# A seven-product feed-forward on one Trainium2 core: PSUM banks, weight sums and modulation steps in another order

## The chip, the core and the metric

The kernel runs on one core of a Trainium2 chip. Its engines are TensorE (PE), VectorE (DVE), ScalarE (ACT), GpSimd (POOL) and SyncE (SP), each with an instruction stream of its own; semaphores order them. The metric is the device time of one execution in microseconds. The kernel before took 2130.96 us, the median of three runs from 2126.84 to 2132.02.

## The reference

Two layers, each a half feed-forward, a token mixer, and a second half feed-forward, over 256 latent and 256 context tokens with a model width of 1024 (the last two blocks on the latent tokens alone):

```
swiglu(h, w1, w3, w2) = (silu(h @ w1) * (h @ w3)) @ w2          # 1024 -> 2816 -> 1024
m = (silu(c) @ w_ada[l] + b_ada[l]) in 9 vectors of 1024         # mc likewise, from c_ctx
x = x + 0.5 * m[2] * swiglu(modulate(rms_norm(x), m[0], m[1]), ...)      # feed-forward 0
x = x + m[5] * token_mixer(modulate(rms_norm(x), m[3], m[4]), ...)
x = x + 0.5 * m[8] * swiglu(modulate(rms_norm(x), m[6], m[7]), ...)      # feed-forward 1
```

Everything is float32. The kernel computes a product from a rounded part (hi) and a rest (lo) of either factor: hi x hi, hi x lo and lo x hi.

## The kernel before, in words

**Products.** Activations lie transposed, channels on partitions and tokens along the free axis. A weight block of 512 rows by 256 columns is loaded (512 KB, L297) by SP into one of a few raw buffers, cast to `whi` by ACT (L324), and `wlo` = raw - `whi` is formed by DVE (L325). Three matmuls of 128x256 follow per 128x128 piece.

**Feed-forward over 512 tokens.** `ffn_both` runs three times: layer 0 first, layer 0 second, layer 1 first. Its 11 column blocks of w1 and w3 are done as follows: block 0 in the entry before it, blocks 1 and 2 by `ordinary`, blocks 3 to 10 by `seven`, in groups of one, four and three, each group followed by `down` blocks (products with w2). The `seven` function computes a w1 block and a w3 block together, with seven half-size products instead of eight in the manner of Strassen. Such a pair is seven units, 0 to 6, of 24 matmuls each (L753), 24 pairs in all. The weights of the units are a11, s1, s2, a12, s3, s4, a22: three raw blocks, two sums which the DMA forms (s1 and s3, loaded by SP at L725 and accumulated by POOL's queue at L726), and two sums which DVE forms (s2 = s1 + a11 and s4 = s2 + a12, L739).

**Banks of a pair.** The units write the PSUM banks b, c, b, a, b, c, b. Between them a bank is read: ACT keeps b after unit 0 (q1), c after unit 1 (p5) and b after unit 2 (w1), all at L758; DVE adds a to q1 after unit 3, b to p5 after unit 4 and c to w1 after unit 5 (L761); after unit 6 DVE gates (L776). Banks b and c are two halves of one tile `p1`; a is half of a tile `p3`. Dependencies are tracked per tile.

**Order.** The function `pipeline` writes the order of PE, DVE and ACT out by hand. Per unit it emits: evacuations of the unit before (`now`); loads, and casts and subtractions of units up to four ahead (`prep`, where also the two sums stand); pieces of finished modulation vectors (`finish`); modulation steps; ACT's silu or the cast of a finished pair (`end`); then the unit's matmuls. There are five raw buffers, of which units hold at most three at a time.

**Modulation steps.** A vector of `m` and `mc` is computed beside the products by the generator `ada`: eight steps, each a 512 KB load (L224) and two DVE operations that accumulate weights times the two conditioning vectors (L240; the first step L238). Then `ada_end` sums over partitions with four ones-matmuls (L253), copies the row (L257), transposes it (L260) and adds the bias (L262). Steps are spread by each unit's `cost`: 0.14 for a pair's unit, 0.6 for a unit of the second ordinary block, 0.3 per 128 rows in `down`. `ffn_both` does 32, 40 and 40 steps in its three runs. The first `down` block of the first two runs has a `need`: the eight steps of the first vector must be done before its residual add.

**The last feed-forward** (`ffn`, 256 tokens) takes its products one after the other, in an order which the scheduler makes.

Of the kernel before, what the change touches and what calls it, by code (L numbers as in the profile page):

```python
# [79 lines left out]
def dit_kernel(ctx: ExitStack, tc: tile.TileContext, I: dict, out: bass.AP):  # L80
# [44 lines left out]
    xr = [z0[:, t * D:(t + 1) * D] for t in range(3)] + [z1[:, 0:D]]  # L125
    junk, dg = z1[:, D:2 * D], z1[:, 2 * D:2 * D + 512].rearrange("p (t c) -> p t c", t=4)
    c32 = z1[:, 2 * D + 512:2 * D + 768].rearrange("p (k c) -> p k c", k=KD)
    qrow, ms4 = z1[:, 2 * D + 768:2 * D + 896], z1[:, 2 * D + 896:2 * D + 908].rearrange("p (a t) -> p a t", a=3)
    last_wada = half_zone(0)[:, 0:D].rearrange("p (k m c) -> p k m c", k=2, m=2)
# [119 lines left out]

    def ada_end(l, m, acc, pool):  # L250
        pa = psum_bg(f"pa{l}_{m}")
        for q in range(4):
            te.matmul(pa[32 * q:32 * q + 32, 0, :], ones32, acc[:, q % 2, (q // 2) * 512:(q // 2 + 1) * 512],  # L253
                      start=True, stop=True, tile_position=(0, 32 * q))
        yield
        mrow = pool.tile([P, 512], F32, tag="mrow", name="mrow")
        v.tensor_copy(mrow, pa[:, 0, :])  # L257
        yield
        for b in range(4):
            te.transpose(pa[:, 1, b * P:(b + 1) * P], mrow[:, b * P:(b + 1) * P], ident)  # L260
        yield
        v.tensor_tensor(modT[l][:, m].rearrange("p (h b) t -> p h b t", h=2),  # L262
                        pa[:, 1, :].rearrange("p (b h t r) -> p h b t r", b=4, h=2, t=2)[:, :, :, :, 0],
                        biasT[l][:, 8 * m:8 * m + 8].rearrange("p (h b) -> p h b", h=2).unsqueeze(3)
                        .to_broadcast([P, 2, 4, 2]), ALU.add)
        modulated(l, m)

# [345 lines left out]
    class Unit:  # L613


        def __init__(self, mm, prep, load=None, takes=0, gives=0, now=(), end=(), cost=1.0, need=None):
            self.mm, self.prep, self.load, self.takes, self.gives = mm, prep, load, takes, gives
            self.now, self.end, self.cost, self.need = now, end, cost, need

    def pipeline(units, fills, steps, total, made):  # L620

# [16 lines left out]
        with tc.manual_schedule(engines={eng.PE, eng.DVE, eng.Activation}):  # L638
            for i in range(len(units) + 1):
# [8 lines left out]
                while pi < min(len(units), i + 4):  # L648
                    while li < len(units) and (li <= pi or out + units[li].takes <= 3):
                        if units[li].load:  # L650
                            units[li].load()
                        out += units[li].takes
                        li += 1
                    units[pi].w = units[pi].prep()
                    out -= units[pi].gives
                    pi += 1
                for f in fills.get(i, ()):
                    f()
                finish()
                if i < len(units):  # L660
                    want += units[i].cost * scale
                    while did < min(total, int(want + 1e-6)) and step():
                        did += 1
                if prev:
                    for f in prev.end:
                        f()
                if i < len(units):
                    units[i].mm(units[i].w)
# [44 lines left out]
    def seven(fm, wa, wb, c0, fp, done):  # L713
# [22 lines left out]
        def summed(name, a, b):  # L736
            def prep():
                x[name] = fm.sum_place()
                v.tensor_tensor(x[name], x[a], x[b], ALU.add)  # L739
                return split(x[name], 4, 2 * P)  # L740
            return prep

        def part(bank, form, first=False):
            def mm(wt):
                if bank == "b" and first:
                    x["q1"], x["p5"], x["w1"] = fm.places()
                    pab, pc = psum("p1"), psum_bg("p3")
                    x["b"], x["c"], x["a"] = pab[:, 0], pab[:, 1], pc[:, 0]
                for k in range(4):
# [23 lines left out]
        def gate(h, by):  # L773
# [4 lines left out]

        cost = 0.14
        return [  # L780
            Unit(part("b", fm.b11, True), whole("a11"), first_loads, 1, 0, [keep("q1", "b")], cost=cost),
            Unit(part("c", fm.t1, True), whole("s1"), None, 0, 0, [keep("p5", "c")], cost=cost),
            Unit(part("b", fm.t2), summed("s2", "s1", "a11"), None, 0, 1, [keep("w1", "b")], cost=cost),
            Unit(part("a", fm.b21, True), whole("a12"), raw("a12", wa, 1), 1, 0, [add("q1", "a")], [silu(0, "q1")], cost=cost),
            Unit(part("b", fm.t3), whole("s3"), None, 0, 0, [add("p5", "b")], cost=cost),
            Unit(part("c", fm.b22), summed("s4", "s2", "a12"), None, 0, 1, [add("w1", "c")], [silu(1, "w1")], cost=cost),
            Unit(part("b", fm.t4), whole("a22"), raw("a22", wb, 1), 1, 1, [gate(0, "b"), gate(1, "p5")],
                 [lambda: done(x["gt"])], cost=cost)]

    def ffn_both(l, f, norm, mods, then, first):  # L790

# [4 lines left out]
        with tc.tile_pool(name=f"ffn{l}{f}", bufs=1) as fp:  # L796
# [27 lines left out]
            def ordinary(c):  # L824
# [17 lines left out]
                for n, (w, name) in enumerate(((w1, "p1"), (w3, "p3"))):  # L842
                    for i in range(2):
                        more = {"cost": 0.6 if c > 1 else 0}
# [6 lines left out]
                return us  # L851

            def down(cg, r0, kt, last, need):
# [18 lines left out]
                for k in range(0, kt, 4):  # L872
                    n = min(4, kt - k)
                    more = {"cost": 0.3 * n}
                    if k + n == kt:
                        more.update(now=[added], end=[stats] if last else [], need=need)
                    us.append(chunk(w2, r0 + k, n, cg * 2 * P, acc, k == 0, k + n == kt,
                                    lambda k=k: (g["hi"], g["lo"], k), **more))
                return us

# [15 lines left out]
            with norm.done():  # L896
                pipeline(units, fm.fills, ada(mods, fp, made), KD * len(mods), made)
# [4 lines left out]
    def ffn(l, f, norm, then):  # L902

# [3 lines left out]
        with tc.tile_pool(name=f"ffn{l}{f}", bufs=1) as fp:  # L907
            def weights(n):
                return [tuple(fp.tile([P, 4, 2 * P], F32R, name=f"e{i}{x}") for x in ("hi", "lo")) for i in range(n)]

            for g0, g1 in ((0, 6), (6, 11)):
                ghi, glo = (zone(i, F32R).rearrange("p (k n) -> p k n", k=12) for i in range(2))
                for g in range(g0, g1):
# [613 lines left out]
```

## Time and profile before

| | |
|---|---|
| median of three runs | 2130.96 us |
| profiled execution, its own time | 2139.14 us |
| its span, first to last instruction | 2137.4 us |
| PE busy | 1978.2 us (93%) |
| DVE busy | 1580.8 us (74%) |
| ACT busy | 962.6 us (45%) |
| mean granted TensorE clock | 0.979 |
| moved by DMA | 326.49 MB, mean 153 GB/s |

The profile is of one execution, and its times are relative to the span's start. Busy time counts an engine with any instruction under way. A granted clock of 1 is 2.4 GHz and of 0.5 is 1.2 GHz. In the timelines a matmul's length overlaps the next one's, so the time per matmul is read from the distance of their starts. The idle time in square brackets is what an engine waited before an instruction, with the instruction that released it.

### The profile page before, as it was taken

The page shows a single profiled execution, that of the slowest core. Times are in us where ns is not written, and L with a number is a line of the kernel's source. Part 1 is how long each engine was busy: PE and PEld are TensorE (multiplying, and loading weights), DVE is VectorE, ACT ScalarE, POOL GpSimd, SP SyncE. Part 2 cuts the span into 40 slices and gives each one's busy share as a digit, 9 for nine tenths or more (in the row PEclk, how much of TensorE's full clock was granted, in tenths as well). Part 3 has the DMA queues.
Part 4 walks back from the last instruction along what each step waited for, and adds up shares of the span by engine and source line. Part 5 has one row for each costly group of instructions (what it writes and reads, how often), then busy time and mean ns, then how long its engine had stood idle before and what let it go on. Part 6 is the DMA issues. An engine that isn't in the chain of part 4 may idle for free. (4 is left out here: it accounts for less than half of the span.)

```text
span 2137.4 us, 32048 instructions
## 1 busy us (share of the span) xinstructions
PE 1978.2 (93%) x12743; PEld 1733.8 (81%) x12743; DVE 1580.8 (74%) x2338; ACT 962.6 (45%) x1466; POOL 116.4 (5%) x80
## 2 busy tenths in 40 slices
PE   8979898899999999998889899988988999999998
PEld 6768887788777778876887778777878798899998
DVE  6776776767678877787678777776877769967555
ACT  3423423356466533531432444324334567766443
POOL 1100100000001110000000000000000000110000
PEclk8989999999999999999999999999999999999999
DMA  8765765432212545665677365766763333455663
GB/s 296 209 165 156 171 198 137 121 120 83 79 57 88 164 149 162 159 177 165 164 194 197 94 183 118 213 163 164 210 160 116 89 98 114 142 172 180 186 188 108
DMA packets 278542, 326.49 MB, mean 153 GB/s; under 512 B 15520, under 2 KB 260344, under 8 KB 278136
## 3 DMA queue, kind: packets, MB, share of 16 engines
q1 hardware_dynamic: 253048, 299.27, 45.3%
q0 software_dynamic: 25344, 25.17, 8.1%
q8 instruction: 100, 1.64, 0.3%
q14 instruction: 50, 0.41, 0.1%
HBM read 321.25 MB, written 3.15 MB: 152 GB/s over the span
## 5 line engine op out<-in xcount | busy, mean ns | idle before, releaser
L324 ACT CAST whi<-wraw 128x1024 fp32r<-128x1024 f32 (+2 forms) x371 | 369.8, 1000 | 569.9 <-PE py L320 220.2
L325 DVE TENSOR_TENSOR wlo<-wraw,whi 128x1024 fp32r<-128x1024 f32 (+2 forms) x343 | 403.2, 1178 | 193.6 <-ACT whi L324 188.7
L240 DVE SCALAR_TENSOR_TENSOR aacc<-wada,cs,aacc 128x1024 f32<-128x1024 f32 x224 | 280.4, 1298 | 4.6 <-DMA wada<-w_ada 4.5
L753 PE MATMUL p<-hhi_f,whi 128*128 128x256 f32 x768 | 222.3, 289 | 47.4 <-DVE half L761 26.4
L753 PE MATMUL p<-zone,whi 128*128 128x256 f32 x1152 | 212.8, 287 | 43.1 <-ACT half L758 43.1
L753 PEld LDWEIGHTS p<-zone,whi 128*128 128x128 f32 x1152 | 179.7, 194 | 52.7 <-ACT half L758 52.7
L319 PE MATMUL p<-hhi_f,whi 128*128 128x256 f32 (+1 forms) x672 | 216.2, 322 | 2.3 <-DVE hhi_f L392 2.3
L753 PE MATMUL p<-hlo_f,whi 128*128 128x256 f32 x768 | 217.3, 283 | 0.0
L753 PE MATMUL p<-hhi_f,wlo 128*128 128x256 f32 x768 | 217.0, 283 | 0.0
L321 PE MATMUL p<-hhi_f,wlo 128*128 128x256 f32 (+1 forms) x672 | 215.0, 320 | 1.1 <-DVE wlo L325 0.6
L320 PE MATMUL p<-hlo_f,whi 128*128 128x256 f32 (+1 forms) x672 | 215.5, 321 | 0.5 <-DVE hlo_f L397 0.2
L753 PEld LDWEIGHTS p<-hhi_f,whi 128*128 128x128 f32 x768 | 148.4, 193 | 62.4 <-DVE half L761 31.1
L319 PE MATMUL py<-ghi,whi 128*128 128x512 f32 x492 | 194.4, 395 | 0.0
L320 PE MATMUL py<-glo,whi 128*128 128x512 f32 x492 | 192.8, 392 | 0.6 <-DVE glo L325 0.5
L321 PE MATMUL py<-ghi,wlo 128*128 128x512 f32 x492 | 192.1, 391 | 0.0
L753 PE MATMUL p<-zone,wlo 128*128 128x256 f32 x576 | 162.7, 282 | 0.0
L753 PEld LDWEIGHTS p<-hlo_f,whi 128*128 128x128 f32 x768 | 148.6, 194 | 0.2
L753 PEld LDWEIGHTS p<-hhi_f,wlo 128*128 128x128 f32 x768 | 148.6, 193 | 0.0
L319 PEld LDWEIGHTS p<-hhi_f,whi 128*128 128x128 f32 x672 | 128.5, 191 | 14.0 <-issue 3.5
L321 PEld LDWEIGHTS p<-hhi_f,wlo 128*128 128x128 f32 x672 | 127.0, 189 | 12.1 <-POOL wlo L325 1.2
L320 PEld LDWEIGHTS p<-hlo_f,whi 128*128 128x128 f32 x672 | 127.2, 189 | 11.6 <-DVE hlo_f L397 1.6
L319 PE MATMUL pg<-hhi_m,whi 128*128 128x512 f32 (+1 forms) x384 | 132.2, 344 | 0.0
(363 smaller groups left out, 4381.3 us busy)
## 6 DMA issues: line engine op xcount, KB each, us to landing
wraw<-ffn_w SPq DMA_DIRECT2D x232, 512.0 KB, 4.2
wada<-w_ada SPq DMA_DIRECT2D x128, 512.0 KB, 3.6
wraw<-w_in SPq DMA_DIRECT2D x64, 512.0 KB, 3.5
s<-ffn_w SPq DMA_DIRECT2D x48, 512.0 KB, 5.2
s<-ffn_w POOLq DMA_DIRECT2D x48, 512.0 KB, 6.8
wraw<-w_out SPq DMA_DIRECT2D x16, 512.0 KB, 3.5
wada<-w_ada SPq DMA_DIRECT2D x30, 256.0 KB, 5.7
wraw<-w_in SPq DMA_DIRECT2D x16, 384.0 KB, 3.3
```

The costliest lines, as they stand in the source:

```text
L240: v.scalar_tensor_tensor(acc[:, t], w, cs[:, k, t:t + 1], acc[:, t], op0=ALU.mult, op1=ALU.add)
L319: te.matmul(o, a, xh, start=start, stop=False)
L320: te.matmul(o, a, xl, start=False, stop=False)
L321: te.matmul(o, b, xh, start=False, stop=stop)
L324: s.copy(hi, src)
L325: eng.tensor_tensor(lo, src, hi.bitcast(F32), ALU.subtract)
L753: te.matmul(om, wt[w][:, k, cm], form[f][:, k], start=(first and k == m == n == 0), stop=(k == 3 and m == 1 and n == 2), skip_group_check= ...
```

## The change

The following is done at once.

- In a pair bank b has a tile `p1` of its own, and c and a are the halves of tile `p3`.
- The two sums of a pair are no longer part of `prep`: they are emitted as `first` in the slot after the units of that slot were prepared, so one slot ahead of their cast.
- In a slot `end` of the unit before stands ahead of the steps. In a pair only unit 2 has a cost (1), the second ordinary block's units have 1, `down` 0.22 per 128 rows.
- `ada_end` yields twice before its ones-matmuls.
- A `down` block with `need` hands its residual add to the first unit of the next block.
- The runs of `ffn_both` do 32 steps each. Vector (1,7) is computed on PE in the third run by the new `ada_apart`, with two of its steps per slot: fp32 matmuls of the two conditioning columns with the weights, at four column positions. Vector (1,8) is done in the last feed-forward, one step after each product.

```diff
     def ada_end(l, m, acc, pool):
+        yield
+        yield
         pa = psum_bg(f"pa{l}_{m}")
...
+    def ada_apart(l, m, pool, made):
+        pa = psum_bg(f"pa{l}_{m}")
+        v.memset(pa[:, 0, 0:L], 0.0)
+        ahead = ada_load(l, m, 0)
+        yield
+        for k in range(KD):
+            w, ahead = ahead, ada_load(l, m, k + 1) if k + 1 < KD else None
+            for q in range(4):
+                te.matmul(pa[32 * q:32 * q + 2, 0, 0:L], cs[:, k], w[:, q * L:(q + 1) * L],
+                          start=(k == 0), stop=(k == KD - 1), tile_position=(0, 32 * q))
+            if k == KD - 1:
+                made.append(ada_apart_end(l, m, pa, pool))
+            yield
+
+    def ada_apart_end(l, m, pa, pool):
+        mrow = pool.tile([P, 512], F32, tag="mrow", name="mrow")[:, 0:L]
+        v.tensor_copy(mrow, pa[:, 0, 0:L])
+        yield
+        for b in range(2):
+            te.transpose(pa[:, 1, b * P:(b + 1) * P], mrow[:, b * P:(b + 1) * P], ident)
+        yield
...
@@ pipeline
+                if pi < len(units) and units[pi].first:
+                    units[pi].first()
                 for f in fills.get(i, ()):
                     f()
                 finish()
+                if prev:
+                    for f in prev.end:
+                        f()
                 if i < len(units):
                     want += units[i].cost * scale
                     while did < min(total, int(want + 1e-6)) and step():
                         did += 1
-                if prev:
-                    for f in prev.end:
-                        f()
-                if i < len(units):
+                    for _ in range(2):
+                        next(apart, None)
                     units[i].mm(units[i].w)
@@ seven
         def summed(name, a, b):
-            def prep():
+            def add():
                 x[name] = fm.sum_place()
                 v.tensor_tensor(x[name], x[a], x[b], ALU.add)
-                return split(x[name], 4, 2 * P)
-            return prep
+            return add
...
-                    pab, pc = psum("p1"), psum_bg("p3")
-                    x["b"], x["c"], x["a"] = pab[:, 0], pab[:, 1], pc[:, 0]
+                    pb, pac = psum("p1"), psum_bg("p3")
+                    x["b"], x["c"], x["a"] = pb[:, 0], pac[:, 0], pac[:, 1]
...
-        cost = 0.14
+        cost = 0
...
-            Unit(part("b", fm.t2), summed("s2", "s1", "a11"), None, 0, 1, [keep("w1", "b")], cost=cost),
+            Unit(part("b", fm.t2), whole("s2"), None, 0, 1, [keep("w1", "b")], cost=1, first=summed("s2", "s1", "a11")),
...
-            Unit(part("c", fm.b22), summed("s4", "s2", "a12"), None, 0, 1, [add("w1", "c")], [silu(1, "w1")], cost=cost),
+            Unit(part("c", fm.b22), whole("s4"), None, 0, 1, [add("w1", "c")], [silu(1, "w1")], cost=cost,
+                 first=summed("s4", "s2", "a12")),
@@ down, in ffn_both
-                    more = {"cost": 0.3 * n}
-                    if k + n == kt:
-                        more.update(now=[added], end=[stats] if last else [], need=need)
+                    more = {"cost": 0.22 * n}
+                    if k + n == kt and need is None:
+                        more.update(now=[added], end=[stats] if last else [])
...
+                if need is not None:
+                    late.append((added, need))
+                elif late:
+                    us[0].now, us[0].need = [late[0][0]], late.pop()[1]
@@ ffn
                             product(acc, load(w, KD, g * 2 * P), (hhi, hlo), L)
+                            with norm.done():
+                                background(1)
@@ the blocks
-    ffn_both(0, 1, after, [(0, 8)] + [(1, m) for m in range(4)], entry, True)
+    ffn_both(0, 1, after, [(0, 8)] + [(1, m) for m in range(3)], entry, True)
...
-    ffn_both(1, 0, entry, [(1, m) for m in range(4, 9)], after, False)
+    ffn_both(1, 0, entry, [(1, m) for m in range(3, 7)], after, False, (1, 7))
...
-    ffn(1, 1, entry, Output())
+    ffn(1, 1, entry, [(1, 8)], Output())
```

The first place where the order differs is PE's stream in a pair of the first feed-forward. The rows are the first matmuls of units 0 to 6, with what each writes (`p1` or `p3`) and reads; the rest of a unit is left out.

Before:

```order
L753 MATMUL p1_2955<-hhi_f00_129,whi_2843 128x256 [waits Activation_49]
...
L753 MATMUL p1_2955<-zone0_614,whi_2874 128x256 [waits Activation_49]
...
L753 MATMUL p1_2955<-zone0_614,whi_2904 128x256 [waits Activation_49]
...
L753 MATMUL p3_2956<-hhi_f00_129,whi_2947 128x256 [waits PE_49]
...
L753 MATMUL p1_2955<-zone0_614,whi_2982 128x256 [waits Activation_49]
...
L753 MATMUL p1_2955<-hhi_f00_129,whi_3012 128x256 [waits DVE_49]
...
L753 MATMUL p1_2955<-hhi_f00_129,whi_3043 128x256 [waits DVE_49,Activation_49]
```

After:

```order
L785 MATMUL p1_2955<-hhi_f00_129,whi_2847 128x256 [waits Activation_49]
...
L785 MATMUL p3_2956<-zone0_614,whi_2878 128x256 [waits Activation_49]
...
L785 MATMUL p1_2955<-zone0_614,whi_2908 128x256 [waits Activation_49]
...
L785 MATMUL p3_2956<-hhi_f00_129,whi_2947 128x256 [waits Activation_49]
...
L785 MATMUL p1_2955<-zone0_614,whi_2982 128x256 [waits Activation_49]
...
L785 MATMUL p3_2956<-hhi_f00_129,whi_3012 128x256 [waits DVE_49]
...
L785 MATMUL p1_2955<-hhi_f00_129,whi_3047 128x256 [waits DVE_49,Activation_49]
```

Six of the seven units wrote the tile `p1`; now the units write `p1` and `p3` in turn.

The second place is DVE's stream from the end of this pair into the next: `half` and `w1` are the places of the kept banks and of the sums, `aacc` the accumulator of a modulation vector.

Before:

```order
L761 TENSOR_TENSOR half1_617<-p1_2955,half1_617 128x512 [waits PE_49]
L325 TENSOR_TENSOR wlo_3106<-s1_2939,whi_3105 128x1024 [waits DMASW6_49,Activation_49]
L761 TENSOR_TENSOR w1_618<-p1_2955,w1_618 128x512 [waits PE_49]
L739 TENSOR_TENSOR half1_617<-s1_2939,wraw_2942 128x1024
L325 TENSOR_TENSOR wlo_3136<-half1_617,whi_3135 128x1024 [waits Activation_49]
L240 SCALAR_TENSOR_TENSOR aacc_2669<-wada_2908,cs_116,aacc_2669 128x1024 [waits DMAHW1_49]
L240 SCALAR_TENSOR_TENSOR aacc_2669<-wada_2908,cs_116,aacc_2669 128x1024
L776 SCALAR_TENSOR_TENSOR gt_3078<-p1_2955,gt_3078 128x2x256 [waits PE_49]
```

After:

```order
L793 TENSOR_TENSOR half1_617<-p1_2955,half1_617 128x512 [waits PE_49]
L355 TENSOR_TENSOR wlo_3110<-s1_2939,whi_3109 128x1024 [waits DMASW6_49,Activation_49]
L772 TENSOR_TENSOR half1_617<-s1_2939,wraw_2942 128x1024
L793 TENSOR_TENSOR w1_618<-p3_2956,w1_618 128x512 [waits PE_49]
L355 TENSOR_TENSOR wlo_3140<-half1_617,whi_3139 128x1024 [waits Activation_49]
L808 SCALAR_TENSOR_TENSOR gt_3082<-p1_2955,gt_3082 128x2x256 [waits PE_49]
...
L772 TENSOR_TENSOR half0_616<-half1_617,wraw_3045 128x1024
L355 TENSOR_TENSOR wlo_3236<-half0_616,whi_3235 128x1024 [waits PE_49,Activation_49]
L240 SCALAR_TENSOR_TENSOR aacc_2635<-wada_3016,cs_116,aacc_2635 128x1024 [waits DMAHW3_49]
```

The sum stands ahead of the add of unit 5 instead of behind it, and the step has left the place ahead of the gate for the slot behind the subtraction of the next pair's s4.

The third place is the start of the third `ffn_both` in the changed kernel: on DVE the gating of block 0 (L924), the subtraction of the fourth weight block (L355) and the new memset.

```order
L924 TENSOR_TENSOR gt_11078<-gt_11078,p3_10816 128x1024 [waits PE_49,Activation_49]
L355 TENSOR_TENSOR wlo_11118<-wraw_11103,whi_11117 128x1024 [waits DMAHW3_49,Activation_49]
L273 MEMSET pa1_7_11121 128x256
L355 TENSOR_TENSOR glo_11082<-gt_11078,ghi_11081 128x1024 [waits Activation_49]
```

On PE, where the matmuls of the entry (L351) went over into those of block 1 (L349) without others between:

```order
L351 MATMUL p3_10816<-hhi_f10_10660,wlo_10683 128x256
L279 MATMUL pa1_7_11121<-wada_11123,cs_116 2x256 [waits DMAHW2_49,DVE_49]
L279 MATMUL pa1_7_11121<-wada_11123,cs_116 2x256 x3
L349 MATMUL p1_11131<-hhi_f10_10660,whi_11099 128x512 [waits Activation_49]
```

Four matmuls of the vector now stand ahead of block 1, and the first of them waits for the memset on DVE.

## Rows read from the trace of the kernel before

**Rows 1.** The page, part 1: busy time, share of the span and instructions of each engine.

```profile
PE 1978.2 (93%) x12743; PEld 1733.8 (81%) x12743; DVE 1580.8 (74%) x2338; ACT 962.6 (45%) x1466; POOL 116.4 (5%) x80
```

**Rows 2.** Waits of PE: line waited for, us in total, times, longest.

```profile
PE p L753 <- ACT half L758: 43.1, 47, 4.4
PE p L753 <- DVE half L761: 26.4, 23, 2.6
PE pa L253 <- DVE aacc L240: 24.5, 14, 5.2
PE p L753 <- DVE w L761: 21.0, 24, 0.9
```

**Rows 3.** Windows, the nine groups of pairs; columns in the row ahead of them.

```profile
core 0: us, PE busy (x) PEld busy (x) DVE busy (x) ACT busy (x) POOL busy (x), PEclk, DMA share, GB/s
...
1006.00:1106.50 100.50, 85.49 (x680) 82.40 (x678) 65.47 (x66) 41.69 (x50) 9.08 (x7) 0.96 0.71 174
...
sum 601.00, PE 508.85 PEld 487.94 DVE 414.54 ACT 254.76 POOL 44.10; mean PE 56.54 PEld 54.22 DVE 46.06 ACT 28.31 POOL 4.90
```

**Rows 4.** Timeline of PE in pairs: start, length, instruction, idle before it.

```profile
1066.82 0.28 PE L753 MATMUL p<-hhi_f,whi 128*128 128x256 f32 x1
...
1069.43 0.28 PE L753 MATMUL p<-hhi_f,wlo 128*128 128x256 f32 x1
...
1074.65 0.38 PE L753 MATMUL p<-hhi_f,whi 128*128 128x256 f32 x1 [2.23 <-DVE half L761]
...
1075.95 0.41 PE L753 MATMUL p<-hhi_f,whi 128*128 128x256 f32 x1
...
1078.51 0.41 PE L753 MATMUL p<-hhi_f,whi 128*128 128x256 f32 x1
```

**Rows 5.** Timeline of DVE in the same pair.

```profile
1058.19 1.22 DVE L325 TENSOR_TENSOR wlo<-wraw,whi 128x1024 fp32r<-128x1024 f32 x1
1059.39 1.22 DVE L325 TENSOR_TENSOR glo<-gt,ghi 128x1024 fp32r<-128x1024 f32 x1
...
1062.37 1.22 DVE L739 TENSOR_TENSOR half<-half,wraw 128x1024 f32<-128x1024 f32 x1
1064.91 1.23 DVE L325 TENSOR_TENSOR wlo<-half,whi 128x1024 fp32r<-128x1024 f32 x1 [1.32 <-ACT whi L324]
...
1069.79 2.48 DVE L240 SCALAR_TENSOR_TENSOR aacc<-wada,cs,aacc 128x1024 f32<-128x1024 f32 x2
1072.18 0.68 DVE L761 TENSOR_TENSOR half<-p,half 128x512 f32<-128x512 f32 x1
1072.78 1.22 DVE L325 TENSOR_TENSOR wlo<-wraw,whi 128x1024 fp32r<-128x1024 f32 x1
1073.91 0.69 DVE L761 TENSOR_TENSOR half<-p,half 128x512 f32<-128x512 f32 x1
```

**Rows 6.** Timeline of PE at the first ones-matmuls and transposes of a vector.

```profile
149.38 3.03 PE L253 MATMUL pa<-aacc,ones 128*32 128x512 f32 x8 [5.24 <-DVE aacc L240]
153.21 1.12 PE L260 MATMUL pa<-k_ident,mrow 128*128 128x128 f32 x4 [0.80 <-DVE mrow L257]
```

**Rows 7.** Windows around two waits of the ones-matmuls.

```profile
147.10:157.30 10.20, 7.12 (x20) 3.79 (x21) 6.88 (x11) 0.00 (x0) 0.00 (x0) 0.50 0.45 147
...
1246.00:1250.00 4.00, 3.76 (x10) 1.01 (x11) 4.00 (x7) 1.05 (x1) 0.00 (x0) 0.57 0.78 221
```

**Rows 8.** Instructions of line 207: durations in ns min/median/max, first and last start.

```profile
L207 PE MATMUL pa<-wada,zone x240: 272/273/423, 14.2 to 43.1; 128*32 128x128 f32 x120
```

**Rows 9.** Timeline of DVE at the start of the third two-half feed-forward.

```profile
1301.74 1.22 DVE L325 TENSOR_TENSOR wlo<-wraw,whi 128x1024 fp32r<-128x1024 f32 x1
```

**Rows 10.** Timeline of PE at the same place.

```profile
1297.77 0.39 PE L319 MATMUL p<-hhi_f,whi 128*128 128x512 f32 x1
```

**Rows 11.** Window of the last feed-forward; columns as in rows 3.

```profile
1939.50:2137.40 197.90, 190.83 (x1614) 190.11 (x1612) 113.51 (x151) 92.37 (x124) 0.00 (x0) 0.99 0.52 158
```

**Rows 12.** The page, part 6: issues, KB each, us to landing.

```profile
wraw<-ffn_w SPq DMA_DIRECT2D x232, 512.0 KB, 4.2
...
s<-ffn_w POOLq DMA_DIRECT2D x48, 512.0 KB, 6.8
```

More of the change, by code (lines that the diff above doesn't have):

```diff
@@ L126, in dit_kernel @@
     junk, dg = z1[:, D:2 * D], z1[:, 2 * D:2 * D + 512].rearrange("p (t c) -> p t c", t=4)
+    qrow, ms4 = z1[:, 2 * D + 768:2 * D + 896], z1[:, 2 * D + 896:2 * D + 908].rearrange("p (a t) -> p a t", a=3)
     c32 = z1[:, 2 * D + 512:2 * D + 768].rearrange("p (k c) -> p k c", k=KD)
-    qrow, ms4 = z1[:, 2 * D + 768:2 * D + 896], z1[:, 2 * D + 896:2 * D + 908].rearrange("p (a t) -> p a t", a=3)
     last_wada = half_zone(0)[:, 0:D].rearrange("p (k m c) -> p k m c", k=2, m=2)
@@ L265, in ada_end @@
                         .to_broadcast([P, 2, 4, 2]), ALU.add)
+        modulated(l, m)
+    def ada_apart(l, m, pool, made):
[18 more added lines that the diff above has]
+        yield
+        v.tensor_tensor(modT[l][:, m].rearrange("p (q b) t -> p q b t", q=4),
+                        pa[:, 1, 0:L].rearrange("p (b q r) -> p q b r", b=2, q=4)[:, :, :, 0:2],
+                        biasT[l][:, 8 * m:8 * m + 8].rearrange("p (q b) -> p q b", q=4).unsqueeze(3)
+                        .to_broadcast([P, 4, 2, 2]), ALU.add)
         modulated(l, m)
@@ L613, in dit_kernel, with __init__, pipeline @@
     class Unit:
-        def __init__(self, mm, prep, load=None, takes=0, gives=0, now=(), end=(), cost=1.0, need=None):
-            self.mm, self.prep, self.load, self.takes, self.gives = mm, prep, load, takes, gives
+        def __init__(self, mm, prep, load=None, takes=0, gives=0, now=(), end=(), cost=1.0, need=None, first=None):
+            self.mm, self.prep, self.load, self.takes, self.gives, self.first = mm, prep, load, takes, gives, first
             self.now, self.end, self.cost, self.need = now, end, cost, need
-    def pipeline(units, fills, steps, total, made):
+    def pipeline(units, fills, steps, total, made, apart):
         eng = mybir.EngineType
@@ L782, in seven, with ffn_both @@
             Unit(part("c", fm.t1, True), whole("s1"), None, 0, 0, [keep("p5", "c")], cost=cost),
-            Unit(part("b", fm.t2), summed("s2", "s1", "a11"), None, 0, 1, [keep("w1", "b")], cost=cost),
+            Unit(part("b", fm.t2), whole("s2"), None, 0, 1, [keep("w1", "b")], cost=1, first=summed("s2", "s1", "a11")),
             Unit(part("a", fm.b21, True), whole("a12"), raw("a12", wa, 1), 1, 0, [add("q1", "a")], [silu(0, "q1")], cost=cost),
             Unit(part("b", fm.t3), whole("s3"), None, 0, 0, [add("p5", "b")], cost=cost),
-            Unit(part("c", fm.b22), summed("s4", "s2", "a12"), None, 0, 1, [add("w1", "c")], [silu(1, "w1")], cost=cost),
+            Unit(part("c", fm.b22), whole("s4"), None, 0, 1, [add("w1", "c")], [silu(1, "w1")], cost=cost,
+                 first=summed("s4", "s2", "a12")),
             Unit(part("b", fm.t4), whole("a22"), raw("a22", wb, 1), 1, 1, [gate(0, "b"), gate(1, "p5")],
                  [lambda: done(x["gt"])], cost=cost)]
-    def ffn_both(l, f, norm, mods, then, first):
+    def ffn_both(l, f, norm, mods, then, first, extra=None):
         hhi, hlo = norm.hi, norm.lo
@@ L843, in ordinary @@
                     for i in range(2):
-                        more = {"cost": 0.6 if c > 1 else 0}
+                        more = {"cost": 1 if c > 1 else 0}
                         if i and name == "p1":
@@ L851, in ordinary @@
                 return us
+            late = []
             def down(cg, r0, kt, last, need):
@@ L896, in ffn_both @@
             with norm.done():
-                pipeline(units, fm.fills, ada(mods, fp, made), KD * len(mods), made)
+                pipeline(units, fm.fills, ada(mods, fp, made), KD * len(mods), made,
+                         ada_apart(*extra, fp, made) if extra else iter(()))
             for _ in to_residual(w2, 6, (g["hi"], g["lo"]), NTOK, gate, st, fp, weight_places, 16, then, (3,)):
@@ L900, in ffn_both, with ffn @@
         return st
-    def ffn(l, f, norm, then):
+    def ffn(l, f, norm, mods, then):
         hhi, hlo = norm.hi, norm.lo
@@ L909, in weights @@
                 return [tuple(fp.tile([P, 4, 2 * P], F32R, name=f"e{i}{x}") for x in ("hi", "lo")) for i in range(n)]
+            pending[:] = [ada(mods, fp)]
             for g0, g1 in ((0, 6), (6, 11)):
```

## The prediction

> **What bounds the kernel now.** The engine shares come first: TensorE (PE) is busy for 1978.2 of 2137.4 us [rows 1]. An engine at 93% can only be helped where it idles or runs at its low clock, so the next view is PE's waits. Four causes stand far ahead of the rest [rows 2]: 43.1 us for the keep copy of ScalarE (ACT; 47 times) and 26.4 and 21.0 us for the adds of VectorE (DVE; 23 and 24 times), all before matmuls of the seven-product pairs, and 24.5 us of ada_end's ones-matmuls for the accumulator (14 times). The first three make 90.5 us over 24 pairs: almost four stalls in each.
>
> The windows over the nine groups of pairs say what a pair costs: 601.0 us for 24, or 25.0 each [rows 3]. What it would cost without stalls is in PE's timeline. The 24 matmuls of a unit without a stall, of which the first and the last are shown, start from 1066.82 to 1069.43: 23 steps of 0.1135 us [rows 4]. A pair has 7 such units, so 168 x 0.1135 = 19.07 us, and 24 pairs 457.6 us. The excess is 143.4 us: 90.5 of those waits, 52.9 for the rest. Part of the rest is what a stall does after it ends: after the 2.23 us idle at 1074.65 PE starts at the full pitch and then falls to its low level, 12 steps from 1075.95 to 1078.51, 0.213 us each, twice the pitch [rows 4]. These two pitches are TensorE's levels of 2.4 and 1.2 GHz.
>
> **Where the stalls come from.** The names of the PSUM tiles tell it. In the kernel before, banks b and c of a pair are two halves of one tile, and a wait is for the tile. So unit 1, which writes c, waits for the copy out of b that only starts when unit 0 has ended; units 2, 5 and 6 likewise wait for something that follows the unit straight before. For a copy PE idled 0.92 us on the mean (43.1 / 47) [rows 2]; for an add 2.23 us at 1074.65, because on DVE that add, at 1073.91, stood behind the two operations of a step, another add and a subtraction [rows 4, 5].
>
> **The change part by part.**
>
> *Banks in separate tiles.* Now b has its own tile, and c and a share the other, so the units write p1, p3, p1, p3, p1, p3, p1. Each waits for an evacuation of the unit before the last, which has a whole unit of 24 x 0.1135 = 2.72 us to run, against the 0.92 us that a copy kept PE waiting. All four stalls should go. A pair is then bounded by PE's 19.07 us. I take 19.6 (half a us for what is left at the entries and of low clock): 24 x 19.6 = 470.4, and with 8 for the vectors' pieces that fall into the groups (3.03 and 1.12 us at one place, at the low level [rows 6]: some 2 each for four) 478 instead of 601, a gain of 122.
>
> *Is something else late next?* DVE first. Its starts in a pair are 0.6 us apart behind a gate or an add, 1.2 behind a subtraction or a weight sum, 2.4 behind a step (two operations) [rows 5]. A pair has 7 subtractions and 2 sums (10.8), 3 adds and 2 gates (3.0), the subtraction of the gated result (1.2) and now 32/28.28 = 1.13 steps (2.7): 17.7 us. It waits besides, 1.32 us after a sum, for the cast of the same weight on ACT [rows 5]; of the two sums' 2.6 I keep 1.8 before the next part. So DVE needs up to 19.5 us and PE 19.07: level. Transfers next: a group of four pairs has a DMA share of 0.71 over 100.5 us, or 71.4 us at full share, 17.9 per pair [rows 3]. A pair of 19.6 us then has share 0.91. Both are close to PE without passing it; I take 10 us off the gain for transfers that come late at the groups' entries, where raw buffers must be refilled. So 112 us.
>
> The Trainium skill (DMA: Bandwidth & Descriptors, Specifications) gives some 358 GB/s from memory to one core. By that the 4.27 MB of a pair (7 x 512 KB and 1.13 x 512 KB) would take, as an estimate from that page, 11.9 us, the transfers could not bind, and the 10 us above would not be lost: 1996 instead of 2006. The trace differs: 174 GB/s at share 0.71 is 245 at full share [rows 3].
>
> *Weight sums a unit ahead, steps in one slot, `end` ahead of the steps.* The sum now stands on DVE a unit before its cast, so ACT needn't wait for it and DVE not for ACT. The steps come only in the fourth slot, behind the last pending add, so an add has no 2.4 us ahead of it. Counted above: neither adds work. If DVE is late the cover is the four units of weights ahead (10.9 us). On SyncE's queue the step's load stays one of some six per pair.
>
> *The two yields, and the residual of the first down block moved to the next block.* The ones-matmul comes two units (some 5.4 us) after the last step; it waited at most 5.24 us [rows 2, 6]. It is late by then only where DVE itself is. Of 24.5 us I keep 4.5: 20 gained, bounds 12 and 24.5. These stalls have the low level behind them: around 149.38, 10.2 us at 0.50; around 1246, 4.0 us at a mean of 0.57 [rows 7]. A low stretch loses up to half its length: 5.1 us in the first, and 0.43 x 4.0 = 1.7 in the second. The ones-matmuls were waited for 14 times [rows 2]; if three more of them were followed by a stretch like the second, that is 5.1 + 4 x 1.7 = 12. I take 10; bounds 3 (the first of these only in part) and 17.
>
> *Vector (1,7) on PE.* 32 matmuls with four column positions, 256 columns each. Bounds for one: 0.27 us, the duration of the form with 128 columns on the same four positions [rows 8], and 0.095, a quarter of 3.03 / 8 (eight with 512 columns at the low level, overlapping [rows 6]; half the columns, twice the clock). So 3.0 to 8.7 us; I take 3.5, near the second, which is a time per matmul in a row of them. Removed are four ones-matmuls and two transposes of that vector (-1.5); its new transposes wait once for a copy, 0.8 in the old ones [rows 6], so +1. But the first matmul also waits for a memset that stands on DVE behind the fourth subtraction of the entry. In the trace PE goes on at 1297.77 with the next matmuls at once; that subtraction ends at 1302.95 [rows 9, 10]. With some 0.3 for the memset PE would idle 5.4 us, queued behind it the whole first unit, and the low level after it costs some 2.5. Sum +11; bounds +2 (the memset comes before the handover) and +18. It takes 16 DVE operations (about 19 us) off that block, which hides them anyway.
>
> *Vector (1,8) in the last feed-forward.* Eight steps beside PE: window 197.9 us with DVE at 113.51 and DMA share 0.52 [rows 11], so 19 us on DVE and 4 MB are hidden. Its ones-matmul is waited for inline, as at 149.38: 5.24 + 0.80 = 6 [rows 6]; bounds 0 and 15 (the loads then also late).
>
> **Sum.** -112 - 20 - 10 + 11 + 6 = -125 us. The profiled execution took 2139.1 us and would take 2014; the runs shown have their median 8.2 below it, 2131.0, so I forecast 2006.
>
> **Rivals.**
> *Pairs become DVE's or the transfers' (22 us a pair).* For: 17.7 to 19.5 us of DVE and 17.9 of transfers against 19.07, and their bursts don't fit exactly; DVE waits for casts. Against: DVE's sums are now ahead, and the loads run four units ahead. 24 x 22 + 8 = 536, a gain of 65 in place of 112: 2053.
> *The change doesn't do what it says.* If a wait were put down for more than its tile (the copies and adds still stand behind the unit before in their engines' order), a pair stays at 25.0 us and only the other terms stay: 2131 - 30 + 17 = 2118. Against: the waits before were 47 on the copy and 47 on adds, just the unit pairs that share the tile.
> *Slower: raw weights late.* A step's load goes to a raw buffer that the pair's loads need too, and with the steps fixed at one place a buffer comes free late; the loads behind it in SyncE's one queue wait. At 4.2 us to landing, 6.8 for the accumulated ones [rows 12], this decides only when the pair gets over 25.0 + 13/24 = 25.5 us, that is, when each pair waits 6.4 us for weights. With 27 us: 2131 - 13 + 48 = 2166. Against: 25.5 would be share 0.70, what the DMA has now.
>
> **How the numbers follow.** Forecast 0.62, pairs bound elsewhere 0.24, nothing gained in the pairs 0.06, slower 0.04, and 0.04 for better than 1978 (no loss at the entries, and the vectors at their lower bounds). The forecast's own range is 1978 to 2035: down 10 for the entries, 9 for the memset, 6 for the last block and some of the low clock; up 7 and 9 for the last two and 13 for pairs at 20.1. To hold 8 in 10 the range takes in most of the second case: 1978 to 2060. A measurement of this kernel tells some 0.3% (6.4 us) from no change. Faster 0.94: the first two, the last, and 0.04 of the third; the same 0.02; slower 0.04.
>
> **What would show it.** Right: the waits of pair matmuls on the copy and on the adds nearly gone; nine groups of pairs of about 480 us together, DVE share in a group of four over 0.85 and DMA share about 0.9; no wait of ones-matmuls over 1 us; one wait of some 5 us on the memset at the start of the third feed-forward of 512 tokens; one of some 5 us about eight products into the last feed-forward. Wrong: a new wait of pair matmuls on subtraction or cast (22 us and more per pair), or the old waits at full count.

## The result, and the profile after

The changed kernel took 2029.52 us (median of three runs, 2027.78 to 2037.19) against 2130.96: 0.954 of the time, 95% interval 0.950 to 0.958. On another chip it took 2031.39 (five runs) against 2131.46. The forecast was 2006 in a range of 1978 to 2060: the direction and the range are right, and the gain is 101 us instead of 125. The profiled execution has a span of 2025.9 us.

The gain of 101 us is between medians; the execution profiled before was 8.2 us above its own. In the profile TensorE is busy for 35 us less than before in a span 111.5 us shorter [rows 1]:

```profile
PE 1943.0 (96%) x12797; PEld 1730.5 (85%) x12797; DVE 1556.6 (77%) x2323; ACT 965.5 (48%) x1466; POOL 117.6 (6%) x80
```

Its waits on the page of the changed kernel (line waited for, total, times, longest) answer to [rows 2]:

```profile
PE pa L262 <- DVE mrow L259: 21.9, 8, 5.0
PE p L785 <- DVE half L793: 12.2, 4, 3.6
PE pa L279 <- DVE pa L273: 5.4, 1, 5.4
...
PE p L785 <- ACT half L790: 0.5, 1, 0.5
```

The 90.5 us of the pairs' waits are 12.7 us now, and those of the ones-matmuls (L255 now) are gone. Two entries stand out. One is the memset's 5.4 us, forecast to the tenth. The other is 21.9 us before the transposes (L262) of a vector, for the copy that DVE makes of its row; it was 2.7 us (for L260 there). DVE's own waits say why:

```profile
DVE aacc L238 <- PE pa L255: 44.4, 7, 9.8
```

Before, this wait (for L253 there) was 2.3 us in all. The first step of a vector now waits seven times for TensorE's ones-matmuls of the vector before, 6.3 us on the mean.

The windows of the second run's groups (four pairs, three pairs) and the sum over the nine groups answer to [rows 3]:

```profile
953.10:1039.20 86.10, 82.53 (x686) 81.42 (x685) 69.44 (x72) 43.32 (x51) 9.48 (x8) 0.98 0.79 195
1083.60:1148.80 65.20, 60.23 (x513) 59.98 (x510) 54.97 (x59) 30.62 (x39) 1.30 (x1) 0.95 0.50 134
1269.40:1288.80 19.40, 19.40 (x170) 19.30 (x169) 17.03 (x16) 11.85 (x14) 1.51 (x2) 1.00 0.79 177
...
sum 518.80, PE 490.84 PEld 486.00 DVE 427.11 ACT 257.66 POOL 38.44; mean PE 54.54 PEld 54.00 DVE 47.46 ACT 28.63 POOL 4.27
```

A pair costs 518.8 / 24 = 21.6 us, where the forecast had 19.9 with the vectors' pieces (20.3 with the 10 us that it took off for transfers), and its first rival 22.3. But the single pair at 1269.4 takes 19.4 us, which speaks for TensorE as the bound there. In the group of four DVE's share is 0.81 and the DMA share 0.79, where the forecast named over 0.85 and about 0.9 as signs of being right. Timelines of DVE and of TensorE in a pair of the first run show what happens in the others:

```profile
223.15 2.47 DVE L240 SCALAR_TENSOR_TENSOR aacc<-wada,cs,aacc 128x1024 f32<-128x1024 f32 x2
229.19 1.60 DVE L238 TENSOR_SCALAR aacc<-wada,cs 128x1024 f32<-128x1024 f32 x2 [3.57 <-PE pa L255]
230.71 1.21 DVE L355 TENSOR_TENSOR wlo<-wraw,whi 128x1024 fp32r<-128x1024 f32 x1
231.84 0.68 DVE L793 TENSOR_TENSOR half<-p,half 128x512 f32<-128x512 f32 x1
232.44 1.21 DVE L355 TENSOR_TENSOR wlo<-wraw,whi 128x1024 fp32r<-128x1024 f32 x1
...
240.16 0.68 DVE L259 COPY mrow<-pa 128x512 f32<-128x512 f32 x1
```

```profile
228.06 1.07 PE L255 MATMUL pa<-aacc,ones 128*32 128x512 f32 x8
...
232.57 0.58 PE L785 MATMUL p<-hhi_f,whi 128*128 128x256 f32 x1 [3.45 <-DVE half L793]
```

A vector's last step ends at 225.6. The next vector's first step (L238) follows in the same slot, but overwrites the same accumulator, which the ones-matmuls must read first. These stand two units later on TensorE, at 228.06. DVE does nothing for 3.57 us, and the add that frees TensorE's next bank ends at 232.5, 3.6 us later for it; TensorE idles 3.45 us. At the groups of three the stop comes among the `down` units ahead of them, and TensorE pays for it at the transposes:

```profile
305.93 1.42 DVE L238 TENSOR_SCALAR aacc<-wada,cs 128x1024 f32<-128x1024 f32 x2 [7.98 <-PE pa L255]
...
315.76 0.68 DVE L259 COPY mrow<-pa 128x512 f32<-128x512 f32 x1
```

```profile
316.50 1.10 PE L262 MATMUL pa<-k_ident,mrow 128*128 128x128 f32 x4 [4.97 <-DVE mrow L259]
```

DVE waits 7.98 us, makes the row copy late, and TensorE waits 4.97 us for it.

### The profile page after: what moved, and what is told of

It reads as the page before. It is cut to its first block, busy times and chain, and to the rows that moved or that the text cites. A ratio compares the mean times of both kernels' runs of the same rounds, so it can differ in the third digit from the quotient of the medians.

```text
span 2025.9 us, 32128 instructions
## 1 busy us (share of the span) xinstructions
PE 1943.0 (96%) x12797; PEld 1730.5 (85%) x12797; DVE 1556.6 (77%) x2323; ACT 965.5 (48%) x1466; POOL 117.6 (6%) x80
## 5 line engine op out<-in xcount | busy, mean ns | idle before, releaser
L355 DVE TENSOR_TENSOR wlo<-wraw,whi 128x1024 fp32r<-128x1024 f32 (+2 forms) x343 | 402.3, 1176 | 159.4 <-ACT whi L354 154.5
L240 DVE SCALAR_TENSOR_TENSOR aacc<-wada,cs,aacc 128x1024 f32<-128x1024 f32 x210 | 264.6, 1298 | 1.7 <-DMA wada<-w_ada 1.7
L349 PE MATMUL p<-hhi_f,whi 128*128 128x256 f32 (+1 forms) x672 | 216.9, 323 | 2.4 <-DVE hhi_f L422 2.4
L351 PE MATMUL p<-hhi_f,wlo 128*128 128x256 f32 (+1 forms) x672 | 214.8, 320 | 3.1 <-DVE wlo L355 2.6
L785 PE MATMUL p<-zone,whi 128*128 128x256 f32 x1152 | 207.4, 283 | 0.5 <-ACT half L790 0.5
L349 PE MATMUL py<-ghi,whi 128*128 128x512 f32 x492 | 193.9, 394 | 0.0
L351 PE MATMUL py<-ghi,wlo 128*128 128x512 f32 x492 | 192.9, 392 | 0.0
L349 PEld LDWEIGHTS p<-hhi_f,whi 128*128 128x128 f32 x672 | 128.0, 190 | 17.3 <-issue 5.7
L351 PEld LDWEIGHTS p<-hhi_f,wlo 128*128 128x128 f32 x672 | 128.0, 190 | 14.3 <-DVE wlo L355 3.0
L349 PE MATMUL pg<-hhi_m,whi 128*128 128x512 f32 (+1 forms) x384 | 132.1, 344 | 0.0
```

What stands on the lines that cost most here:

```text
L240: v.scalar_tensor_tensor(acc[:, t], w, cs[:, k, t:t + 1], acc[:, t], op0=ALU.mult, op1=ALU.add)
L349: te.matmul(o, a, xh, start=start, stop=False)
L351: te.matmul(o, b, xh, start=False, stop=stop)
L355: eng.tensor_tensor(lo, src, hi.bitcast(F32), ALU.subtract)
L785: te.matmul(om, wt[w][:, k, cm], form[f][:, k], start=(first and k == m == n == 0), stop=(k == 3 and m == 1 and n == 2), skip_group_check= ...
```

## The experiments

Theory 1 was that the missing gain went to this one accumulator. Its rival, theory 2, was the forecast's own first rival: pairs bound by all the work of DVE or by the transfers. Times are medians; ratios are to the kernel before on the same chip.

**The changed kernel again**, for comparison on the same chip.

> The changed kernel as it is, for comparison on the same chip. Both theories: 2029 us within 6, nine groups of pairs together about 519 us, VectorE's first steps of a vector waiting some 44 us in 7 places for the ones-matmuls.

Measured 2031.39 us (ratio 0.952, 0.949 to 0.954), groups of pairs 519.2 us (here and below from the first to the last pair matmul of each of the nine groups), DVE's wait 44.4 us.

**The vector's first step held back.**

```diff
-        want = 0.0
+        want, ended = 0.0, -9
...
-                    while did < min(total, int(want + 1e-6)) and step():
+                    while did < min(total, int(want + 1e-6)) and (did % KD or i >= ended + 3) and step():
                         did += 1
+                        ended = ended if did % KD else i
```

> The changed kernel, but a vector's first step waits at least three slots after the last step of the vector before, by when the ones-matmuls that read the same accumulator stand ahead of it on TensorE. Theory 1 (the pairs lost to the one accumulator: VectorE stands still until TensorE reaches the ones-matmuls two units on, and then is late with adds, subtractions and row copies): VectorE's wait of 44 us falls below 20, the pairs' wait of 12.2 us for the add below 3, the transposes' wait of 21.9 us below 10, the groups of pairs fall from 519 to about 495 us, the time by 15 to 25 us to some 2008. Theory 2 (pairs are bound at about 21.5 us by the whole work of VectorE or the transfers): VectorE's wait falls, but the groups stay above 510 us and the time within 6 us of 2029.

Measured 2000.07 us (0.939, 0.937 to 0.941), 31 us less than the changed kernel on that chip. TensorE's waits:

```profile
PE pa L262 <- DVE mrow L259: 15.6, 10, 2.8
PE pa L279 <- DVE pa L273: 5.4, 1, 5.4
...
PE p L786 <- DVE half L794: 2.9, 3, 2.0
```

No wait of L238 for the ones-matmuls is left, the groups take 490.3 us, and the gain is beyond what theory 1 asked for. Only the order of some steps was moved here, none was taken away: theory 2 falls. The transposes' wait stays at 15.6 us, above the forecast 10: the copy is still one slot ahead of them, behind two operations of the first step and a step.

**Without the two yields.**

```diff
     def ada_end(l, m, acc, pool):
-        yield
-        yield
         pa = psum_bg(f"pa{l}_{m}")
```

> The changed kernel without the two yields ahead of the ones-matmuls, so these follow the last step by one slot. Theory 1: VectorE's wait for the ones-matmuls falls from 44 to under 20 us and with it the pairs' and transposes' waits (34 us together, to under 15), but the ones-matmuls wait for VectorE again, 10 to 20 us in all; the time within 10 us of 2029. Theory 2: the old waits of the ones-matmuls come back (about 20 us) and nothing is gained: 2045 to 2055.

Measured 1998.51 us (0.938, 0.936 to 0.940). Both theories expected the ones-matmuls' old wait back, and so a time near 2029 or above it. It came back with 8.8 us only:

```profile
PE pa L253 <- DVE aacc L240: 8.8, 7, 2.1
PE pa L277 <- DVE pa L271: 5.4, 1, 5.4
PE pa L260 <- DVE mrow L257: 4.6, 6, 2.0
```

```profile
DVE aacc L238 <- PE pa L253: 3.5, 3, 1.2
```

TensorE is busy for less time with the same 12797 matmuls:

```profile
PE 1931.1 (97%) x12797; PEld 1712.5 (86%) x12797; DVE 1557.7 (78%) x2323; ACT 964.6 (48%) x1466; POOL 116.6 (6%) x80
```

Of the 28.9 us between the two profiled spans (2025.9 and 1997.0) 11.9 are busy time, at a mean granted clock of 0.993 against 0.982, and 17.0 idle time. So more than waiting was lost to the yields: two fifths of it is the same work taking longer at a lower granted clock.

The windows of the first pair, of the second run's groups of four and three, and the sum show what is left of a pair:

```profile
101.40:126.50 25.10, 21.34 (x170) 20.95 (x169) 23.65 (x39) 11.66 (x15) 2.60 (x2) 0.93 0.85 225
...
945.60:1029.00 83.40, 81.00 (x686) 78.88 (x685) 69.37 (x72) 43.23 (x51) 9.43 (x8) 1.00 0.81 199
1074.00:1131.50 57.50, 57.50 (x508) 57.50 (x507) 49.12 (x53) 31.14 (x39) 2.59 (x2) 1.00 0.53 143
...
sum 487.80, PE 476.82 PEld 469.65 DVE 412.36 ACT 258.96 POOL 41.98; mean PE 52.98 PEld 52.18 DVE 45.82 ACT 28.77 POOL 4.66
```

Three pairs take 57.5 us, 19.16 each, with TensorE busy throughout and at full clock: the 19.07 us of the forecast. The 30 us that the nine groups take above 24 x 19.07 stand elsewhere: 6 in the first pair (25.1 us) and some 7 in each group of four, where a vector's pieces and waits are among the pairs.

**One yield.**

```diff
     def ada_end(l, m, acc, pool):
         yield
-        yield
         pa = psum_bg(f"pa{l}_{m}")
```

> The changed kernel with one of the two yields ahead of the ones-matmuls. Theory 1 (each slot of delay blocks VectorE's next vector for one unit more, and is too long already): VectorE's wait for the ones-matmuls between 3.5 us (none) and 44 us (two), about 15 to 25, the time between: 2005 to 2020. Rival (one slot is the best of both, since the ones-matmuls' 8.8 us of waiting without yields go as well): 1990 to 1998.

Measured 1995.52 us (0.936, 0.933 to 0.938; runs from 1990.86 to 2000.52), no different from none. DVE waits 15.5 us:

```profile
DVE aacc L238 <- PE pa L254: 15.5, 7, 4.3
```

The wait is where theory 1 put it, but the time is the rival's. TensorE's own waits tell why it comes out even:

```profile
PE pa L261 <- DVE mrow L258: 10.0, 9, 2.0
...
PE p L784 <- DVE half L792: 2.9, 4, 2.0
```

The 8.8 us before the ones-matmuls are gone. In their place 10.0 us instead of 4.6 stand before the transposes, and 2.9 instead of 0.6 before the adds. With the second yield DVE's single waits grow from at most 4.3 to 9.8 us, and these two waits of TensorE to 34 us. TensorE pays for only part of DVE's waiting, probably because DVE has a lead over it; that lead was not measured.

**The vector on TensorE later.**

```diff
-                    for _ in range(2):
+                    for _ in range(2 if i > 3 else i == 0):
                         next(apart, None)
```

> The changed kernel, with the memset of the vector on TensorE in slot 0 as before but its matmuls from slot 4 on. The forecast's term: the wait of 5.4 us at the start of the third feed-forward of 512 tokens goes, and 2 us of low clock behind it: 2029 - 7 = 2022. Rival (the entry is late anyway, and the time comes back as a wait for the cast or subtraction of block 1): a wait of over 3 us stands within the first units there, and the time stays within 3 us of 2029.

Measured 2050.10 us (0.962, 0.960 to 0.964): 19 us slower than the changed kernel, where 7 less was expected. The memset's wait is gone, and this stands in its place:

```profile
PE pa L279 <- DMA wada<-w_ada: 26.5, 4, 9.8
```

Four of the vector's eight steps wait for their load: 6.25, 9.84, 6.57 and 3.84 us. In the longest wait TensorE stands still from 1245.34. A load that lands at 1255.13, just before the matmuls at 1255.18, was issued only at 1251.75. That issue, and then SyncE's own waits from 1225 to 1285:

```profile
1251.75 0.33 SPq L224 DMA_DIRECT2D wada<-w_ada  x1
```

```profile
SPq L224 <- PE pa L279: 21.0, 7, 6.1
SPq L224 <- DMA wada<-w_ada: 16.1, 6, 4.0
SPq L224 <- DVE aacc L240: 7.4, 2, 5.9
```

So most of that wait lay ahead of the issue: SyncE waits for the vector's own matmuls and for DVE's steps, which read the loaded buffers, and for earlier loads of the same kind. In the changed kernel it waits for the vector's matmuls too, 17.8 us from 1205 to 1250, and TensorE does not notice. One difference is that there the vector's matmuls are over at 1246.74, before DVE's first step of this run at 1251.92; here DVE's steps begin at 1235.04 and need loads of the same kind in the same slots. That this is the cause was not tested. The rival expected another wait, of another kind.

**The split alone**, on the kernel before.

```diff
-                    pab, pc = psum("p1"), psum_bg("p3")
-                    x["b"], x["c"], x["a"] = pab[:, 0], pab[:, 1], pc[:, 0]
+                    pb, pac = psum("p1"), psum_bg("p3")
+                    x["b"], x["c"], x["a"] = pb[:, 0], pac[:, 0], pac[:, 1]
```

> The kernel before with one part of the change alone: bank b in a tile of its own, c and a sharing the other. Theory 1 (the shared tile is what held the pairs; VectorE and the transfers fit beside 19.1 us): the 90.5 us of waits fall below 25, the groups of pairs from 602 to about 510 us, the time to 2030 to 2050. Rival (sums ahead of their cast and the steps' fixed slot are needed too, because an add behind two steps is late in any case): waits of pair matmuls for VectorE stay above 35 us, the groups above 540, the time 2065 to 2090.

Measured 2045.93 us (0.961, 0.957 to 0.966): 84 us of the 101. The groups of pairs take 502.7 us. Of the pairs' three causes in [rows 2] two are small and the third, the add to `w`, is gone; the ones-matmuls wait 29.4 us, somewhat more than before:

```profile
PE pa L253 <- DVE aacc L240: 29.4, 12, 5.7
PE p L753 <- DVE half L761: 6.4, 7, 1.5
PE p L753 <- ACT half L758: 5.7, 5, 1.3
```

Theory 1 holds. The groups are 98 us shorter than in [rows 3], more than the 84 by the medians: the execution profiled before was 8.2 us above its median and this one, of 2042.78 us, 3.2 below.

**The change with the old banks.** The same two lines the other way round.

> The changed kernel with the banks as before (b and c in one tile, a in the other), all else changed. Theory 1: the waits of pair matmuls come back with 80 us or more, the groups of pairs go from 519 to about 590 to 600 us, the time to 2095 to 2115. Rival (with sums ahead and fixed steps the shared tile would cost little): under 2075.

Measured 2116.65 us (0.994, 0.992 to 0.996), a little above what was expected. The waits of [rows 2] are back:

```profile
PE p L785 <- ACT half L790: 34.7, 45, 3.9
PE p L785 <- DVE half L793: 31.5, 24, 5.0
PE p L785 <- DVE w L793: 20.1, 23, 0.9
```

34.7, 31.5 and 20.1 us; the groups take 608.7 us. Without the split the rest of the change, the costly yields among it, gives 13 us.

**No yields, and the sums in `prep` again.**

```diff
-            Unit(part("b", fm.t2), whole("s2"), None, 0, 1, [keep("w1", "b")], cost=1, first=summed("s2", "s1", "a11")),
+            Unit(part("b", fm.t2), summed("s2", "s1", "a11"), None, 0, 1, [keep("w1", "b")], cost=1),
```

(and s4 likewise, with `summed` as it was)

> The changed kernel without the two yields (1998.5 us) and with the weight sums in the preparation of their unit again, straight before their cast. Theory 1 (VectorE had 17.7 us of work and up to 1.8 us of waiting for casts in a pair of 19.1, so it fits, barely, with the sums as before): VectorE waits about 1.2 us more in each of 48 places, the groups of pairs stay within 8 us of 488, the time within 8 us of 1998.5. Rival (VectorE is the bound then): groups above 505 us, time above 2015.

Measured 2015.85 us (0.947, 0.943 to 0.951), 17 us above the kernel without yields (19 by the two ratios); groups 501.5 us, 13.6 more. The time is the rival's, the groups lie between the two expectations. The pairs wait more for the adds, 5.4 us in place of 0.6:

```profile
PE p L784 <- DVE half L792: 5.4, 8, 0.9
```

So the sums ahead are worth 17 to 19 us. That DVE's whole work bounds the pairs without them is not shown.

**No yields, and the vectors where they were.**

```diff
-    ffn_both(0, 1, after, [(0, 8)] + [(1, m) for m in range(3)], entry, True)
+    ffn_both(0, 1, after, [(0, 8)] + [(1, m) for m in range(4)], entry, True)
...
-    ffn_both(1, 0, entry, [(1, m) for m in range(3, 7)], after, False, (1, 7))
+    ffn_both(1, 0, entry, [(1, m) for m in range(4, 9)], after, False)
...
-    ffn(1, 1, entry, [(1, 8)], Output())
+    ffn(1, 1, entry, [], Output())
```

> The changed kernel without the two yields, and with vectors (1,3), (1,7) and (1,8) where they were: 40 steps on VectorE in each of the second and third feed-forward of 512 tokens, none on TensorE, none in the last feed-forward. By the forecast's two terms (+11 and +6) undoing the moves gains up to 17 us: 1982 to 1992, since 1.41 steps a pair make VectorE's work 18.4 of 19.1 us. Rival (VectorE is then late in the pairs): groups of pairs of the second and third feed-forward together over 10 us above 325, the time 2000 to 2015.

Measured 2010.50 us (0.942, 0.940 to 0.944), 12 us slower than with the moves, or 8 by the two ratios. The groups of the second and third run take 337.1 us against 321.3; the pairs wait for DVE again:

```profile
PE p L783 <- DVE half L791: 12.0, 5, 3.4
```

The spans of the two profiled executions differ by only 5.5 us (2002.5 and 1997.0), so some 10 of these 15.8 us come back outside the pairs.

**No yields, and the memset early.**

```diff
+            next(apart, None)
             for i in range(len(units) + 1):
...
-                    for _ in range(2):
+                    for _ in range(2 if i else 1):
                         next(apart, None)
```

> The changed kernel without the two yields, and with the memset and the first load of the vector on TensorE emitted ahead of the first units' preparation, one of its steps in slot 0 and two in each later slot. From the waits: 5.4 us of the memset go, and 2 us of low clock: 1998.5 - 7 = 1991. Rival (as where its matmuls came later, they wait for their loads behind the weights' on SyncE's queue): waits for the loads of over 5 us, 1998 or more.

Measured 1998.76 us (0.938, 0.935 to 0.941), no different from 1998.51. The memset's wait is gone, and waits for the loads take 3.4 us of it:

```profile
PE pa L277 <- DMA wada<-w_ada: 3.4, 2, 2.6
```

The time is the rival's, with smaller waits than it asked for; the gain of 7 us did not come. The 2 us that are left can't be told from the spread of these runs (1995.95 to 2000.27).

So the versions with the yields gone or halved, or with the first step held back, beat both kernels, by some 30 us over the changed one and 131 to 138 over the one before.

## Why the prediction was right or wrong

**Banks in separate tiles: right, mostly in size.** Forecast -112 us in the pairs. Alone the split takes the groups from 601.0 [rows 3] to 502.7 us, -98, and the time down by 84; with the rest of the change but without the yields the groups are at 487.9, -113. The tile names in the order had told which waits would go, and three pairs of 19.16 us each are what the pitch of 0.1135 us had told. That this comes so near to the forecast's -112 is in part luck: the forecast put 0.5 us on every pair and 10 on the groups' entries, and the runs have most of it in the groups of four.

**The two yields: the step that failed.** The forecast had "20 gained" and 10 of clock behind it. The ones-matmuls' waits did go, 24.5 us to none. But the working asked only who waits for the ones-matmuls, not who waits for their reading. The accumulator has one buffer, so delaying its reader delays the next vector's first writer, on DVE, with all adds, subtractions and copies of the pair queued behind it. That cost 44.4 us on DVE and 34 us before adds and transposes on TensorE. Taking the yields out gains 33 us against the changed kernel on the same chip (2031.39 to 1998.51): in place of a gain of 30 they cost 33. The two numbers have different starting points, since without the yields 8.8 of the 24.5 us of waits were left and the other parts had taken the rest. The residual's move, which stands in the same term, was not run alone.

**Sums, slots and `end`: undervalued.** The forecast said that they add no work and gave them no term of their own; DVE's waits for casts, which they were to end, stood in the working with 1.8 us a pair. The sums ahead are worth 17 us when the yields are out; the steps' fixed slot and `end` were not run alone. Here the forecast was lucky. Taken as they stand, the yields' term was off by some 63 us and the whole sum by 24 (125 against 101), so some 40 us were gained that were not counted, the moves' return below among them. The range was wide enough for the first rival too, so that the time fell into it proves neither.

**Vector (1,7) on TensorE: the wait exact, the return left out.** 5.36 us of idle for the memset stood at 1217.67, where it was put:

```profile
1217.67 1.03 PE L279 MATMUL pa<-wada,cs 128*2 128x256 f32 x8 [5.36 <-DVE pa L273]
```

The time for the matmuls was too low: the 32 matmuls are 64 in the trace, x8 in this row for four of them, and take 5.1 us in all in place of 3.5. And that the block "hides them anyway", of the 16 DVE operations taken off, does not fit: with three vectors, (1,3), (1,7) and (1,8), back in their places the pairs of the two runs are 15.8 us longer. Some 10 us come back elsewhere, so the +11 and the +6 were in part real costs, but their return was left out; together the moves gain 8 to 12 us. Which of the three gains it was not separated.

**Vector (1,8) in the last feed-forward: +6 forecast, nothing measured.** The window answers to [rows 11]:

```profile
1828.10:2025.90 197.80, 188.21 (x1625) 186.11 (x1624) 131.41 (x170) 93.11 (x123) 0.00 (x0) 0.98 0.58 179
```

197.8 us against 197.9. Of the vector's pieces only the transposes, at 1891.92, were waited for on TensorE, for 0.51 us; the wait of some 5 us that was named as a sign did not come.

**The rivals.** Pairs at 21.6 us looked like the first rival (22). They were not: neither DVE's work nor the transfers made them, since the same work in another order takes 20.3. The second rival did not come: the waits on copies and adds fell from 90.5 to 12.7 us. Nor did the slower one.

In the group at 945.6 without yields the DMA share was 0.81 at 199 GB/s, which is 246 at full share as before the change [rows 3], and no pair matmul waited for weights. The Trainium skill gives a limit of some 358 GB/s for a core (DMA: Bandwidth & Descriptors, Specifications). No group here reached that rate, so the figure stays unshown. That the loads at the groups' entries cost 10 us is not shown either.

## What to carry to other kernels

When a reader is moved later to spare it a wait, look for the next writer of the buffer that it reads: with a single buffer the wait moves to that writer's engine, and there everything is queued behind it. Such a moved wait can come out even, as with one yield here, or cost 33 us, as with two, so delays of this kind are tried one step at a time. A second buffer for the accumulator would be another way; it was not tried. And a dependency tracked by the tile makes two banks of one tile one resource: names of tiles in the order of an engine show such waits before a trace does.

## What was not expected of the hardware

The loads of a vector's steps landed 3.6 us after their issue at the median, before the change and with the vector on TensorE later, yet there TensorE waited 3.8 to 9.8 us for them: in the longest of these waits 6.4 us had gone by before the load that ended it was issued. And a wait of DVE of 15.5 us in seven places left the time as it was without any yield, TensorE's waits merely changing places, while 44.4 us in the same seven cost about 33.
